# The first two matrices of a batched matmul loaded as one DMA of 4 KB runs each, instead of two DMAs of 2 KB and 6 KB runs

## Chip, cores, metric

One core of a Trainium2 chip. The metric is the device time of one execution in microseconds; lower is better. "Faster" and "slower" mean over 2%.

## The reference

```python
batch, m, k, n = 16, 512, 512, 512
a: [batch, k, m] float32      b: [batch, k, n] float32
np.matmul(a.transpose(0, 2, 1), b).astype(np.float32)
```

## The kernel before

Each matrix is 1 MB. The sync engine (SP) issues all transfers into one queue that is served by 16 DMA engines. The first batch element is loaded alone so that compute can start early, and each of its two matrices comes in two DMAs: the top 128 rows, one 2 KB row for a partition, then the other 384 rows, three rows (6 KB) for a partition. The second element follows in 8 KB runs, the rest in pairs of elements, 2 MB a DMA, 16 KB runs. VectorE casts to bf16, TensorE multiplies, ScalarE evicts, and SP issues the stores after the loads. Cut to the parts that matter:

```python
in0_v = [x.rearrange("batch (p r) m -> batch p r m", r=RV) for x in (a, b)]          # RV = 4
top_v = [x[0][0:P].rearrange("p m -> p () m") for x in (a, b)]                        # P = 128
low_v = [x[0][P:K].rearrange("(p r) m -> p r m", r=RV - 1) for x in (a, b)]
# ... (cut: tiles and semaphores)
for j in range(2):
    nc.sync.dma_start(x_ts[j][:, 0:1, :], top_v[j]).then_inc(s_f[j], 16)
    nc.sync.dma_start(x_ts[j][:, 1:RV, :], low_v[j]).then_inc(s_f[j], 16)
for j in range(2):
    nc.sync.dma_start(x_ts[j][:, RV:R, :], in0_v[j][1]).then_inc(s_x[j], 16)
for n in range(2, 2 * pairs):
    if n >= NX:                                     # NX = 4 input buffers
        nc.sync.wait_ge(s_in, n - NX + 1)           # wait until the buffer has been cast
    # ... (cut: the load of matrix pair n; the last one in two halves, s_h and s_x)
nc.sync.wait_ge(s_h, 16)
for i in range(pairs - 1):
    nc.sync.wait_ge(s_out, i + 1)
    nc.sync.dma_start(out_v[i], o_ts[i % NO][:]).then_inc(s_o if i else s_o0, 16)

for u in range(G):                                  # the first two batch elements
    if u:
        nc.vector.wait_ge(s_mm, H)
    for j, bf_ts in enumerate((abf_ts, bbf_ts)):
        nc.vector.wait_ge(s_x[j] if u else s_f[j], 16 if u else 32)
        nc.vector.tensor_copy(
            out=bf_ts[0][:], in_=x_ts[j][:, u * RV:(u + 1) * RV, :]
        ).then_inc(s_cast, 1)
        # ... (cut)
# ... (cut: later casts, matmuls, evictions, last store)
```

Any order of the 512 rows over partitions and slots is right, as long as a and b use the same one, because the rows are summed over.

## Time and profile before

| | kernel before |
|---|---|
| time, median of 3 runs | 123.50 us (123.36 to 123.52) |
| span of the profiled execution | 122.1 us (its time 123.84) |
| share of DMA engines' time taken | 97.3% |
| cast of the first a / first b starts | 5.82 / 8.95 us |
| first matmul | 10.47 us |
| last landing of the first b | 8.93 us |

The lines of the profile are shown in the prediction. Some words: a run of memory is a contiguous piece that is moved in one go, and a packet is the record of one such move on one DMA engine. A stall is the time by which a packet lasts longer than is usual for its size. A DMA is issued when SP starts it, and lands when its last share has been counted; the line is what has been issued and not yet moved. A reload is a load into an input buffer that is used a second time. In tables of windows the two last columns are the busy share of the DMA engines and the GB/s that they moved; GB/s times a window of 1 us gives kB.

### The profile page before, as it was taken

How to read it: one execution, taken by the hardware profiler on the slowest of the kernel's cores; microseconds unless marked ns; L12 is line 12 of the kernel's file. 1: busy time of each engine (PE TensorE's matmuls, PEld its weight loads, DVE VectorE, ACT ScalarE, POOL GpSimd, SP SyncE). 2: the span in 40 equal slices, each digit the busy share in tenths (PEclk: the TensorE clock that was granted, in tenths of full speed). 3: DMA queues.
4: the chain of work that ended last, by engine and by line, in shares of the span. 5: the costliest groups of instructions: out<-in, count | busy, mean ns of one | idle time of the engine just before them, and what ended most of it. 6: DMA issues, size and time to landing. Idle time of an engine off the chain costs nothing.

```text
span 122.1 us, 1209 instructions
## 1 busy us (share of the span) xinstructions
PE 62.1 (51%) x480; PEld 35.0 (29%) x480; DVE 38.1 (31%) x48; ACT 32.2 (26%) x41; POOL 0.2 (0%) x4
## 2 busy tenths in 40 slices
PE   0005928379969749979919928989900000000000
PEld 0002304035546325636606605646500000000000
DVE  0033070680494092474356437492000000000000
ACT  4000332400570840091470290091570000000000
POOL 0000000000000000000000000000000000000000
PEclk9999999959999985999999999999997555555555
DMA  2999999999999999999999999999999999999993
GB/s 86 375 411 429 454 429 435 435 440 435 429 429 429 429 429 429 429 429 435 429 429 435 429 429 416 421 429 427 427 421 429 427 429 427 429 429 424 427 429 145
DMA packets 5200, 50.33 MB, mean 412 GB/s; under 512 B 464, under 2 KB 464, under 8 KB 976
## 3 DMA queue, kind: packets, MB, share of 16 engines
q1 hardware_dynamic: 5200, 50.33, 97.3%
HBM read 33.55 MB, written 16.78 MB: 412 GB/s over the span
## 4 chain that ended last, share of the span: by engine, by line
DMA 43%; DVE 7%; ACT 3%; PE 3%; issue 3%; ACTq 0%
DMA x<-in_b_dram 37%; DMA out_dram<-o 6%; DVE abf L117 4%; ACT o L180 3%; DVE bbf L117 3%; PE ps L135 3%; DVE done L123 0%; ACTq L72 0%
## 5 line engine op out<-in xcount | busy, mean ns | idle before, releaser
L155 PE MATMUL ps<-bbf,abf 64*128 64x512 bf16 x448 | 52.9, 393 | 13.1 <-PEq L150 13.1
L155 PEld LDWEIGHTS ps<-bbf,abf 64*128 64x128 bf16 x448 | 31.2, 113 | 34.8 <-issue 20.0
L180 ACT COPY o<-ps 128x1024 f32<-128x1024 f32 x28 | 26.3, 1026 | 40.5 <-PE ps L155 36.5
L117 DVE CAST abf<-x 128x2048 bf16<-128x2048 f32 x14 | 17.1, 1224 | 17.4 <-PE ps L155 13.3
L117 DVE CAST bbf<-x 128x2048 bf16<-128x2048 f32 x14 | 17.1, 1225 | 14.2 <-DMA x<-in_b_dram 14.2
L135 PE MATMUL ps<-bbf,abf 128*128 128x512 bf16 x32 | 9.2, 451 | 13.2 <-PEq L133 13.2
L135 PEld LDWEIGHTS ps<-bbf,abf 128*128 128x128 bf16 x32 | 3.8, 123 | 18.1 <-issue 16.1
L174 ACT COPY o<-ps 128x1024 f32<-128x1024 f32 x4 | 4.1, 1014 | 17.2 <-PE ps L135 17.2
L98 DVE CAST abf<-x 128x2048 bf16<-128x2048 f32 x2 | 2.5, 1227 | 11.7 <-PE ps L135 5.9
L98 DVE CAST bbf<-x 128x2048 bf16<-128x2048 f32 x2 | 2.5, 1225 | 1.9 <-DMA x<-in_b_dram 1.9
L185 ACT ACTIVATE done<-done 1x1 uint32<-1x1 uint32 x8 | 1.6, 196 | 0.0
L174 ACT ACT_TABLE_LOAD x1 | 1.3, 1283 | 0.9 <-SPq L72 0.9
L123 DVE MEMSET done<- 1x1 f32 x14 | 0.8, 59 | 0.0
L102 DVE MEMSET done<- 1x1 f32 x2 | 0.1, 59 | 0.0
L207 POOL MEMSET const-bfloat16-1.0<- 128x1 bf16 x1 | 0.1, 102 | 0.0
L207 POOL MEMSET const-uint8-127<- 128x1 uint8 x1 | 0.1, 102 | 0.0
L207 POOL MEMSET const-float32-0.0<- 128x1 f32 x1 | 0.1, 99 | 0.2 <-issue 0.2
L207 POOL MEMSET const-float32-1.0<- 128x1 f32 x1 | 0.1, 99 | 0.0
## 6 DMA issues: line engine op xcount, KB each, us to landing
out_dram<-o SPq DMA_DIRECT2D x8, 2048.0 KB, 21.8
x<-in_a_dram SPq DMA_DIRECT2D x7, 2048.0 KB, 12.1
x<-in_b_dram SPq DMA_DIRECT2D x6, 2048.0 KB, 15.9
x<-in_b_dram SPq DMA_DIRECT2D x3, 1024.0 KB, 13.4
x<-in_a_dram SPq DMA_DIRECT2D x1, 1024.0 KB, 8.6
x<-in_a_dram SPq DMA_DIRECT2D x1, 768.0 KB, 4.4
x<-in_b_dram SPq DMA_DIRECT2D x1, 768.0 KB, 6.6
x<-in_a_dram SPq DMA_DIRECT2D x1, 256.0 KB, 2.8
```

Source lines behind the costliest of these rows:

```text
L98: nc.vector.tensor_copy(out=bf_ts[0][:], in_=x_ts[j][:, u * RV:(u + 1) * RV, :]).then_inc(s_cast, 1)
L102: nc.vector.memset(dve_done[:, j:j + 1], 0.0).then_inc(s_in, 1)
L117: nc.vector.tensor_copy(out=(bbf_ts if n % 2 else abf_ts)[v][:], in_=x_ts[n % NX][:, v * RV:(v + 1) * RV, :],).then_inc(s_cast, 1)
L123: nc.vector.memset(dve_done[:, n:n + 1], 0.0).then_inc(s_in, 1)
L135: mm = nc.tensor.matmul(ps_ts[0][h][:, t % 2, :], a_m[:, r, t], bbf_ts[0][:, r, :], start=(r == 0), stop=(r == RV - 1),)
L155: mm = nc.tensor.matmul(ps_ts[g][h][:, t % 2, :], a_m[:, t], bbf_ts[v][rows, r, :], start=(v == 0 and r == 0), stop=(v == V - 1 and r == R ...
L174: nc.scalar.copy(out=o_ts[0][:, g, 2 * h:2 * h + 2, :], in_=ps_ts[0][h][:]).then_inc(s_ev[h], 1)
L180: ev = nc.scalar.copy(out=o_ts[i % NO][:, g, 2 * h:2 * h + 2, :], in_=ps_ts[g][h][:])
L185: nc.scalar.memzero(act_done[:, i:i + 1]).then_inc(s_out, 1)
L207: nc = _bacc.Bacc("TRN2", target_bir_lowering=False, num_devices=1)
```

## The change

The intent: no 2 KB packets at the start, two issues and two completions less, and the shorter of the first runs twice as long (2 to 4 KB; the longer ones shrink from 6 to 4 KB). Each matrix is split into an upper and a lower half of 256 rows; a partition takes two rows (4 KB) of each.

```diff
-    top_v = [x[0][0:P].rearrange("p m -> p () m") for x in (a, b)]
-    low_v = [x[0][P:K].rearrange("(p r) m -> p r m", r=RV - 1) for x in (a, b)]
+    first_v = [x[0].rearrange("(h p r) m -> p h r m", h=2, p=P) for x in (a, b)]
...
-            nc.sync.dma_start(x_ts[j][:, 0:1, :], top_v[j]).then_inc(s_f[j], 16)
-            nc.sync.dma_start(x_ts[j][:, 1:RV, :], low_v[j]).then_inc(s_f[j], 16)
+            nc.sync.dma_start(
+                x_ts[j][:, 0:RV, :].rearrange("p (h r) m -> p h r m", h=2), first_v[j]
+            ).then_inc(s_f[j], 16)
...
-                nc.vector.wait_ge(s_x[j] if u else s_f[j], 16 if u else 32)
+                nc.vector.wait_ge(s_x[j] if u else s_f[j], 16)
```

## The prediction

> **What bounds the kernel now.** I read the views in this order: the busy shares and the DMA queue line, the chain of waits, the waits of the queue that issues the transfers, then a table of windows over the first microseconds and the rest. The page says first:
>
> ```profile
> span 122.1 us, 1209 instructions
> PE 62.1 (51%) x480; PEld 35.0 (29%) x480; DVE 38.1 (31%) x48; ACT 32.2 (26%) x41; POOL 0.2 (0%) x4
> DMA  2999999999999999999999999999999999999993
> DMA packets 5200, 50.33 MB, mean 412 GB/s; under 512 B 464, under 2 KB 464, under 8 KB 976
> q1 hardware_dynamic: 5200, 50.33, 97.3%
> ```
>
> No compute engine is busy for much over half the span; the 16 DMA engines are busy for 97.3% of it, and 38 of the 40 slices are full. The traffic is 50.33 MB and cannot shrink. The chain ends like this:
>
> ```profile
> 66.05 13.45 DMA x<-in_b_dram
> 79.50 0.02 issue
> 79.51 7.35 DMA out_dram<-o
> 86.86 0.02 issue
> 86.88 3.76 ACT o L180 x4
> 90.64 0.06 ACTq L72
> ```
>
> The chain stops at 90.64 us, where the last store is issued, but the span ends at 122.1. The landing view gives 30.3 us from issue to landing for that last 2 MB store, which at 429 GB/s needs 4.9 us by itself: the other 25 us it stands in line behind earlier stores. So the chain's casts, matmuls and evictions do not set the end; the amount of work in the DMA line does. Nor does the line run dry earlier: the first reload (issued 17.34 us, landed near 28.4) takes 11 us from issue to landing, of which 4.9 is its own transfer and 1.2 the start-up (first issue 0.94 us, first packet 2.18), so some 5 us of other work still lay ahead of it, and the later ones (up to 19.3 us) have more. A load that is issued a microsecond earlier or later changes nothing at the end. Only these terms count: when the first packet starts, how long each DMA engine then needs for its fixed list of packets, and the last landing.
>
> The change touches the first 2 MB only. The windows there, and after:
>
> ```profile
> 2.00:3.00 1.00, 0.00 (x0) 0.00 (x0) 0.00 (x0) 0.18 (x1) 0.00 (x0) 1.00 0.71 231
> 3.00:4.00 1.00, 0.00 (x0) 0.00 (x0) 0.00 (x0) 0.00 (x0) 0.00 (x0) 1.00 0.99 363
> 4.00:5.00 1.00, 0.00 (x0) 0.00 (x0) 0.00 (x0) 0.00 (x0) 0.00 (x0) 1.00 1.02 422
> 5.00:6.00 1.00, 0.00 (x0) 0.00 (x0) 0.18 (x1) 0.00 (x0) 0.00 (x0) 1.00 1.09 356
> 6.00:7.00 1.00, 0.00 (x0) 0.00 (x0) 1.00 (x1) 0.00 (x0) 0.00 (x0) 1.00 0.89 369
> 7.00:8.00 1.00, 0.00 (x0) 0.00 (x0) 0.04 (x1) 0.00 (x0) 0.00 (x0) 1.00 1.04 430
> 8.00:9.00 1.00, 0.00 (x0) 0.00 (x0) 0.05 (x1) 0.00 (x0) 0.00 (x0) 1.00 1.06 442
> ...
> 24.00:79.00 55.00, 43.93 (x370) 26.06 (x372) 28.00 (x36) 19.10 (x25) 0.00 (x0) 0.94 1.00 430
> 79.00:119.00 40.00, 8.99 (x82) 5.14 (x77) 3.61 (x5) 7.64 (x10) 0.00 (x0) 0.67 1.01 428
> ```
>
> The last column is GB/s, the one before it the busy share. The first packet starts at 2.18, so up to 9.00 the queue has 6.82 us and moves 231+363+422+356+369+430+442 = 2613 kB. At 429 that would take 6.09 us. **0.73 us is all that the beginning loses** against the steady rate, busy share near 1 all the while: packets take longer there, they are not missing. This is the prize, and it is 0.6% of the time.
>
> The trace records each packet too (no view lists them; I counted the records). Undisturbed, one engine starts its next packet 80 ns after a 2 KB packet began, 231 after 6 KB, 306 after 8 KB, and 6 ns after a semaphore packet. The cost fits 4.7 ns + 75.3 ns for each 2 KB. Over that, some packets stall: the second packets of eight engines at the start (208 to 325 ns instead of 84), the first 6 KB packets of a on five engines near 3.0 us (546 to 613 instead of 234), and those of b on seven engines from 5.65 us (416 to 1013). Summed over the medians and divided by 16 engines: 0.12 us in the 2 KB packets, 0.31 us in the 6 KB packets. Most of the rest is that eight of the engines get their first packet 0.26 us after the other eight. Two engines come out late: for b's 6 KB transfer 14 of the 16 landings are in by 8.49 us, the last at 8.93, and on the very last store it is 120.72 against 121.16. Those 0.44 us are carried to the end of the kernel by engines that each have an equal list.
>
> **The Trainium skill.** "DMA: Bandwidth & Descriptors", section "Why small descriptors are slow (HBM only)": a fixed cost of about 3 cycles for each packet. The trace agrees in kind: 4.7 ns a packet here, 6% of a 2 KB one, 2% of a 6 KB one. "Perfetto Trace Analysis", section "DMA Optimizations": merging transfers of small runs, such as 2 KB into 4 or 8 KB, can raise throughput dramatically. This is the intent of the change, but in this trace a 2 KB packet moves 2048 B in 80 ns, so 16 engines 410 GB/s, and only 256 of 5200 packets are of that kind. The first page's section "Latency and other measured facts" has about 600 ns to the first byte of a hardware-issued DMA; here it is 1.24 us from the start of the issue, 0.85 from its end. Its section "Specifications" has 435 GB/s for the fabric and about 358 for a core's share of HBM; the trace holds 428 to 430, so the first is the ceiling here.
>
> **The change part by part.** Two issues go: four of 128 runs become two of 256 runs. An issue costs 0.39 to 0.43 us, and a store with 256 runs (two of 8 KB a partition) shows 0.40 at its cheapest, so the count of runs hardly matters; the later loads are issued about 2 x 0.47 = 0.94 us earlier. They join a full line, so this is worth 0 at the end. Two completion counts go: 2 x 16 semaphore packets, on each engine 2 x 6 = 12 ns, on the path. The packets: each engine carries 8 partitions; before, a partition of one matrix costs 80 + 231 = 311 ns, after it 2 x (4.7 + 150.6) = 311 ns. **The number of runs stays at two in a partition and so does the number of bytes; the longer short run is paid by the shorter long run.** 16 x 0 = 0. Sum of what is certain: -0.01 us.
>
> What is not certain is the stalls. Three of the five starts of a new region (a's lower rows, b's upper and lower) are merged into starts of whole matrices, so the 0.31 us mean of the 6 KB packets, and the 0.44 us of the two late engines, may go in part. Afterwards each matrix still has a first touch of both halves, and the next loads (8 KB) show 0.03 us mean excess, so first touches need not be dear. I choose half: -0.2 us. Against it, if runs are handed out at a fixed pace, the second eight engines get their first packet 0.5 instead of 0.26 us late: +0.1 us for an even chance. Together some -0.15 to -0.2 us.
>
> The first casts should start earlier (a 5.82 to about 5.5 us, b 8.95 to about 8.5), and the first matmul at about 10.0 instead of 10.47. All of this is beside the full DMA line.
>
> **Rivals.** (1) All stalls go with the small and the second transfers: the beginning reaches the steady rate, -0.6 us, 122.9. For it: the stalls sit exactly on the transfers that are merged. Against it: the very first packets stall too, and a start remains. (2) Stalls are as large with two regions half a matrix apart, visited in turn, and the 256 runs start slower: +0.2 to +0.5 us, 123.7 to 124. For it: every engine touches both regions at once; against it: the stores too have two runs a partition, 1 MB apart, and run at 428 GB/s. (3) The earlier first matmul carries through to the end: -0.5 us and more. Against it: the line never runs dry after 2.18 us, and the last store waits 25 us in it. (4) The skill's sentence on small runs taken at face value, a gain in per cent: even free 2 KB packets would give 256 x 80 ns / 16 = 1.3 us, 1%.
>
> **Range and chances.** Before, three runs lie within 0.16 us, so the stalls repeat rather than being chance. 123.5 - 0.2 gives 123.3. No rival that I can size goes past 2.47 us (2%) to either side: the whole startup loss is 0.73 us. Range 122.7 (all stalls gone, and a little) to 123.7 (rival 2, small). Faster by over 2%: 0.01; slower: 0.01; within: 0.98.
>
> **What would show it right or wrong.** Right: 5168 packets, of them 432 under 512 B and 944 under 8 KB; the queue's share still 97%; windows after 9 us at 428 to 430 GB/s; casts of a and b up to half a microsecond earlier without the end following by more than the gain in bytes moved by 9 us. Wrong: a window below 420 GB/s after 10 us, or a first packet later than 2.5 us, or 4 KB packets that take other than some 159 ns, or reloads that now land in under 7 us from their issue, so that the line ran short.

## The result, and the profile after

The changed kernel took 123.48 us (median of 4 runs, 123.31 to 123.61), the kernel before in the same rounds 123.51 (123.36 to 123.54). The ratio is 0.9999, 95% interval 0.9982 to 1.0016: the same. A ratio here is the mean time of one kernel's fast runs over the mean of the other's fast runs of the same rounds, so it is not quite the ratio of the two medians. Executions over 1.5% slower than the fastest of the same kernel are left out of the means.

The profile page of the changed kernel, its span, DMA row, packets and queue share:

```profile
span 121.5 us, 1207 instructions
DMA  2999999999999999999999999999999999999994
DMA packets 5168, 50.33 MB, mean 414 GB/s; under 512 B 432, under 2 KB 432, under 8 KB 944
q1 hardware_dynamic: 5168, 50.33, 97.7%
```

The packet counts are the expected ones: 32 semaphore packets less, and the same number of data packets. The windows of the changed kernel, columns as before:

```profile
2.00:3.00 1.00, 0.00 (x0) 0.00 (x0) 0.00 (x0) 0.18 (x1) 0.00 (x0) 1.00 0.79 152
3.00:4.00 1.00, 0.00 (x0) 0.00 (x0) 0.00 (x0) 0.00 (x0) 0.00 (x0) 1.00 0.93 381
4.00:5.00 1.00, 0.00 (x0) 0.00 (x0) 0.00 (x0) 0.00 (x0) 0.00 (x0) 1.00 1.01 418
5.00:6.00 1.00, 0.00 (x0) 0.00 (x0) 0.13 (x1) 0.00 (x0) 0.00 (x0) 1.00 1.03 422
6.00:7.00 1.00, 0.00 (x0) 0.00 (x0) 1.00 (x1) 0.00 (x0) 0.00 (x0) 1.00 1.02 422
7.00:8.00 1.00, 0.00 (x0) 0.00 (x0) 0.10 (x1) 0.00 (x0) 0.00 (x0) 1.00 1.13 467
8.00:9.00 1.00, 0.00 (x0) 0.00 (x0) 0.64 (x1) 0.00 (x0) 0.00 (x0) 1.00 1.02 434
...
24.00:79.00 55.00, 44.61 (x375) 26.56 (x377) 27.47 (x37) 19.56 (x26) 0.00 (x0) 0.94 1.01 430
```

From 9 us on little differs (435 and 432 GB/s up to 24 us, 430 in both up to 79). Before that, two things moved in opposite directions:

- **The start is slower.** By 3.0 us the change has moved 152 kB, the kernel before 231. The packet records show why: sixteen 4 KB packets start by 2.24 us, eight of them last 661 to 858 ns instead of 159, and the next packet starts at 2.73. Before, packets flow from 2.44 us on; 58 had started by 2.7 us. The 79 kB are 0.18 us at 429 GB/s.
- **The middle is faster.** From 3 to 9 us the change moves 2544 kB, the kernel before 2382 in its first profile. The stalls of the first 6 KB packets are gone: between 3.5 and 9 us no packet lasts over its usual time. The 162 kB are 0.38 us.

So in this pair of profiles the change is ahead by 0.19 us at 9 us. The first a, which takes the slow start in full, is cast at 5.87 us instead of 5.82; b at 8.36 instead of 8.95; the first matmul comes at 9.88 instead of 10.47. The two late engines are gone as well: on the last store all 16 landings lie between 120.17 and 120.59. The other 0.4 us of the span difference (122.1 against 121.5) are about what these late engines were late by (0.44). But the times do not show 0.57 us, so the two profiles had to be doubted first.

### The profile page after: what moved, and what is told of

Read it like the earlier page. It is cut to its first block, busy times and chain, and to the rows that moved or that the text cites. A ratio compares the mean times of both kernels' runs of the same rounds, so it can differ in the third digit from the quotient of the medians.

```text
span 121.5 us, 1207 instructions
## 1 busy us (share of the span) xinstructions
PE 61.9 (51%) x480; PEld 35.1 (29%) x480; DVE 38.1 (31%) x48; ACT 32.2 (26%) x41; POOL 0.2 (0%) x4
## 2 busy tenths in 40 slices
DMA packets 5168, 50.33 MB, mean 414 GB/s; under 512 B 432, under 2 KB 432, under 8 KB 944
## 3 DMA queue, kind: packets, MB, share of 16 engines
q1 hardware_dynamic: 5168, 50.33, 97.7%
## 4 chain that ended last, share of the span: by engine, by line
DMA 59%; DVE 6%; issue 3%; ACT 3%; SPq 2%; ACTq 0%
DMA x<-in_b_dram 53%; DMA out_dram<-o 6%; ACT o L180 3%; DVE bbf L117 3%; DVE abf L117 3%; SPq L77 1%; SPq L73 1%; SPq L83 1%; DVE done L123 0%; ACTq L71 0%; SPq L218 0%; SPq L71 0%
```

## The experiments

Twelve runs follow, of eight further kernels and of the two of the change; each was correct. The main theory, S: the change trades stalls in the middle for a pause at the start, and the pause comes from the 256 runs of the first DMA. One number recurs, the kB moved in windows: "start" is from 2 to 3 us, "by 9" from 2 to 9 us. In some expectations I spoke of "the second eight engines" starting late; the records do not name the engine of a packet, and kB at the start is the sounder measure.

### Again: the changed kernel and the kernel before, unaltered

> The changed kernel once more, for a second profile and more timed rounds. Theory S (the start eats the gain): the change trades the stalls in the middle of the first 2 MB for a dearer start, because 256 runs are handed out more slowly than 128. It expects the second eight engines to get their first packet again about 0.70 us after the first eight (0.26 in the kernel before), the 4 KB packets to stall only in the first microsecond, and the ratio to the kernel before within 0.998 to 1.002. Theory C (chance): the stalls of both kernels are chance and say nothing of the change; it expects them in other places or of other sizes than in the first profile.

Measured: 123.29 us against 123.53; ratio 0.998 (0.9953 to 1.0008). All first sixteen packets last 671 to 922 ns, the seventeenth starts at 2.85 us; start 131 kB, by 9: 2704; no stall over 0.1 us from 3.5 to 9 us. The pause and the calm afterwards repeat; the prediction's even-chance term of 0.1 us was a term that is always there.

> The kernel before, one more look. If the stalls in the middle of its first 2 MB come from its four DMAs for the first matrices, packets stall again at the first 6 KB packets near 3.0 and 5.7 us, by some 0.2 to 0.8 us each, on several engines. If they were chance, they are gone or stand elsewhere. Profiled span 121.5 to 122.4.

Measured: one execution of 123.39 us, span 121.6. Its windows:

```profile
2.00:3.00 1.00, 0.00 (x0) 0.00 (x0) 0.00 (x0) 0.18 (x1) 0.00 (x0) 1.00 0.72 223
3.00:9.00 6.00, 0.00 (x0) 0.00 (x0) 1.98 (x2) 0.00 (x0) 0.00 (x0) 1.00 1.03 412
```

That is 2695 kB by 9 us. Stalls stand at the same places again (3.0 to 3.2, 5.65 to 6.1 us), but smaller: at most 0.26 us there, against 0.78 in the first profile; one of 0.30 us stands elsewhere, at 4.50. No engine left the first loads late: b's last landing came at 8.22 us, and b was cast at 8.24. **So these places belong to the kernel, and the size of the stalls differs from one execution to the next**; the first profile of the kernel before was an unlucky one. By 9 us this execution had moved as much as the changed kernel. Most of the 0.57 us between the first two profiles was not the change.

The very start differs too, and this limits theory S: the first eight packets of the kernel before took 0.63 to 0.64 us here (0.61 with the hold below), where the first profile has 0.08 to 0.10. Long first packets are thus not peculiar to the change. What is peculiar to it is that the other packets wait as well; here they go on from 2.43 us.

> The changed kernel once more, for its ratio on the same chip as the other runs of this call. Pause at the start to 2.7 to 2.9 us, no stalls of over 0.1 us from 3.5 to 9 us, b cast at 8.2 to 8.4 us, ratio to the kernel before 0.997 to 1.000.

Measured: 123.33 us against 123.52; ratio 0.9988 (0.9974 to 1.0003); start 98 kB, by 9: 2671, one stall of 0.20 us where I had expected none over 0.1, b cast at 8.44. The three ratios of the changed kernel, 0.9999, 0.998 and 0.9988, all have intervals that hold 1.

### The size of the runs and their number, apart

> 4 KB runs as in the change, but each matrix in two DMAs of 128 runs (upper and lower half): the run size of the change without its merging. Theory S: the start is as in the kernel before (second eight 0.26 us late), since the first DMA has 128 runs; if the stalls in the middle come from the start of a further DMA, 4 KB packets stall again near 3 and 5.5 us by 0.2 to 0.7 us each, and the ratio is 0.998 to 1.002. Rival: the stalls in the middle came from the mix of 2 KB and 6 KB runs; then none is seen there, and the ratio is 0.995 to 0.998.

```diff
+            for h in range(2):
+                nc.sync.dma_start(
+                    x_ts[j][:, 2 * h:2 * h + 2, :], first_v[j][h]
+                ).then_inc(s_f[j], 16)
```

(in place of the one DMA, with first_v indexed by half, and the wait for 32). The windows of this kernel:

```profile
2.00:3.00 1.00, 0.00 (x0) 0.00 (x0) 0.00 (x0) 0.18 (x1) 0.00 (x0) 1.00 0.97 299
...
5.00:6.00 1.00, 0.00 (x0) 0.00 (x0) 0.54 (x1) 0.00 (x0) 0.00 (x0) 1.00 0.97 291
6.00:7.00 1.00, 0.00 (x0) 0.00 (x0) 0.69 (x1) 0.00 (x0) 0.00 (x0) 1.00 0.99 360
```

Measured: 124.06 us (123.39 to 124.38), ratio 1.0021 (0.9988 to 1.0055). The data packets are those of the change, the same bytes in the same 4 KB runs; a DMA has 128 of them instead of 256, one in a partition instead of two, so their order differs too. The start has 299 kB: **the pause is gone**, 50 packets started by 2.7 us where the change has 16. In its place four packets near 5.0 us stall by 0.96 to 1.5 us, larger than I had expected (0.2 to 0.7), and the window from 5 to 6 us drops to 291 GB/s with the busy share still at 0.97. The mix of 2 KB and 6 KB runs is therefore not what makes packets stall. Nor do longer runs help: this is 4 KB throughout, and it is no faster than 2 KB plus 6 KB.

> First a and b in one DMA each, 512 runs of 2 KB. Theory S paced by the number of runs: the second eight engines start about 1.4 us after the first eight; the packets cost 8 x 4 x 80 = 2.56 us a matrix on an engine instead of 2.49; b is cast at about 9.0 us; ratio 1.002 to 1.008. Rival B, paced by bytes: the second eight start about as late as with 4 KB runs or earlier (0.3 to 0.7 us), ratio 1.000 to 1.003.

```diff
+    first_v = [x[0].rearrange("(r p) m -> p r m", p=P) for x in (a, b)]
...
+            nc.sync.dma_start(x_ts[j][:, 0:RV, :], first_v[j]).then_inc(s_f[j], 16)
```

Measured: 123.94 us (123.86 to 123.95), ratio 1.0027 (1.0 to 1.0054); start 125 kB, by 9: 2590; b cast at 8.95. 31 packets start by 2.48 us, all have ended by 2.56, and the next starts at 2.73. The pause is there with 512 runs, as engines that have nothing to do (busy share 0.37 in this window), and ends at the same time as with 256. So it is not proportional to the count: my 1.4 us failed. It is there with 256 and 512 runs, and not with 128; but those are also the kernels with two and four runs in a partition instead of one, so the count of runs and the form of the DMA are not told apart. The ratio and b's time came as expected.

> First a and b in one DMA each, 128 runs of 8 KB. Theory S with a hand-out paced by the number of runs: the second eight engines start about 0.26 us after the first as in the kernel before, b is cast at about 8.0 us (8.36 after, 8.95 before), the profiled span some 0.3 us under that of the changed kernel, the ratio to the kernel before 0.995 to 0.999. Rival B, paced by bytes or by the first touch of the memory: the second eight start 0.7 to 1.3 us late, nothing is won, ratio 0.999 to 1.004.

```diff
-    first_v = [x[0].rearrange("(h p r) m -> p h r m", h=2, p=P) for x in (a, b)]
...
+            nc.sync.dma_start(x_ts[j][:, 0:RV, :], in0_v[j][0]).then_inc(s_f[j], 16)
```

Measured: 123.26 us, ratio 0.9971 (0.9944 to 0.9998). By 3.0 us 254 kB against the change's 152, so no pause:

```profile
2.00:3.00 1.00, 0.00 (x0) 0.00 (x0) 0.00 (x0) 0.18 (x1) 0.00 (x0) 1.00 0.71 254
3.00:4.00 1.00, 0.00 (x0) 0.00 (x0) 0.00 (x0) 0.00 (x0) 0.00 (x0) 1.00 0.89 352
```

The second line shows what it pays: some forty small stalls of 0.04 to 0.3 us up to 5.7 us. By 9: 2711. b was cast at 8.34 us, where I had expected 8.0. The ratio came as expected, the 0.3 us off the profiled span did not (121.9, in an execution that took 123.62, the slowest of its six).

> One DMA of 128 runs of 8 KB for each first matrix again, beside the changed kernel. If it is better than the change by the pause at the start alone (0.5 us on every engine), its times lie 0.2 to 0.4 us under after_third. If, as in its first run, many small stalls up to 6 us take the place of the pause, both are equal within 0.15 us.

Measured on one chip with the third run of the change: 123.22 us against its 123.33; ratio to the kernel before 0.9976 (0.9961 to 0.9990). The second branch of the expectation holds: the two differ by 0.11 us. It is the best version that I found, 0.3 us under the kernel before in both runs, and by the measure of 2% still the same. Both intervals lie below 1, as the one of the 2 KB runs lies above or at it: from 1024 runs of 2 KB to 256 of 8 KB the time falls by 0.68 us (123.94 to 123.26). By the packet times of the prediction, 64 x 80 against 16 x 306 ns on an engine, an estimated 0.22 us of this is the packets' own cost.

### One part alone

> One part of the change alone: b in one DMA of two 4 KB runs a partition, a in two DMAs of 128 runs of 4 KB (the same order of rows). Theory: no pause at the start, since the first DMA has 128 runs (about 50 packets started by 2.7 us, 16 in the changed kernel), and no stalls of over 0.4 us near 5 us, since b's second DMA is gone; a is cast at about 5.4 us, b at about 8.1, ratio to the kernel before 0.994 to 0.998. Rival: the first packets of b stall whether b comes in one DMA or two, as b's first half did in the kernel with two DMAs each (1.0 to 1.5 us near 5 us); then b is cast at 8.6 us or later and nothing is won over the change.

```diff
+            if j:
+                nc.sync.dma_start(
+                    x_ts[j][:, 0:RV, :].rearrange("p (h r) m -> p h r m", h=2), first_v[j]
+                ).then_inc(s_f[j], 16)
+            else:
+                nc.sync.dma_start(x_ts[j][:, 0:2, :], up_v).then_inc(s_f[j], 16)
+                nc.sync.dma_start(x_ts[j][:, 2:RV, :], dn_v).then_inc(s_f[j], 16)
```

(and the cast of a waits for 32). Measured: 124.36 us (123.28 to 124.98), ratio 1.0069 (1.0031 to 1.0107). The start is the best of all, 377 kB, and a is cast at 5.39 us. But the first packets of b stall near 5.0 us by 0.55 to 0.65 us, four of them, although b comes in one DMA, and b is cast at 8.60. The theory falls: b's second DMA is not what stalls; the rival holds. The profiled execution took 123.51 us; no profile was taken of one near 125, so that these longer ones had larger stalls is likely from the kernel with two DMAs each, but not shown.

### Are later issues to blame?

> The kernel before, with the issue of the two 2 MB loads that follow held until the first b has landed (8.9 us; 2 MB are then still in line, so the line does not run dry). Theory D (a further DMA's start stalls, whatever else is issued): the stalls near 3.0 and 5.7 us stay as they are. Rival I (the stalls come from descriptors of later DMAs being written while the engines work): those near 5.7 us go, the profiled span falls by 0.2 to 0.4 us, ratio 0.997 to 0.999. A ratio above 1.004 would mean that the line ran short.

```diff
+        nc.sync.wait_ge(s_f[1], 32)
         for n in range(2, 2 * pairs):
```

Measured: 123.53 us, ratio 1.0007 (0.9984 to 1.0030). Five packets near 5.65 us stall by 0.28 to 0.86 us although nothing was issued between 3.8 and 8.8 us. Rival I falls for the stalls near 5.65 us; those near 3.0 come while the second element's loads are issued (2.80 to 3.78 us) in this kernel too, and are not tested.

> The changed kernel with everything behind the first a and b held until the first a has landed (5.9 us; b is then still in line). Theory S, in which the 256 runs of the first DMA themselves make the pause at the start: the gap between the first sixteen packets and the next, to about 2.75 to 2.85 us, stays, ratio to before 0.997 to 1.001. Rival I: the pause comes from the issues that follow at 1.9 to 4.1 us, and goes; then a is cast at about 5.3 instead of 5.8 us and the ratio is 0.993 to 0.997.

```diff
+        nc.sync.wait_ge(s_f[0], 16)
         for j in range(2):
             nc.sync.dma_start(x_ts[j][:, RV:R, :], in0_v[j][1]).then_inc(s_x[j], 16)
```

Measured: 123.99 us, ratio 1.0042 (1.0019 to 1.0066). The start has 127 kB and a is cast at 5.92 us: the pause stays, with only a's and b's own DMAs issued. Rival I falls there too. The ratio missed, and usefully: the loads of the second element are issued at 5.9 us, 1.9 us before their turn, and nine of their first packets stall at 7.8 to 8.1 us by 0.13 to 0.46 us; their last landing moves from 13.26 to 13.71 us. With these issues held back the kernel takes 0.4% longer than the kernel before. That the short notice makes the stalls is not shown: in the kernel with two DMAs each, where these loads were issued at 2.80 us, seven of their first packets stall too, by 0.16 to 0.21 us.

### Does the line of transfers alone set the end?

> The changed kernel with the first cast held until the second b has landed (13.3 us instead of 5.9): the first matmul comes some 4.5 us later, at about 14.5. If the line of transfers alone sets the end and has some 5 us of other work ahead of the first reload, as predicted, the time changes by less than 0.3%; the first reload is then issued near 21 us and lands at about the same time as before (27.8 us). If the first casts mattered for the end, the ratio to the kernel before would be up to 1.036.

```diff
+        nc.vector.wait_ge(s_x[1], 16)      # s_x[0] in the other of the two
         for u in range(G):
```

Measured: 126.15 to 130.19 us in four executions, of which two, the profiled one among them, count as slow for their times (the clock is the same, 0.85); the ratio of the two others is 1.0282 (1.0221 to 1.0343), slower. The first reload was issued at 23.65 us, 7.3 us later than in the changed kernel, not the 4.6 I had reckoned, because the stages behind the first matmul moved too. The line had run out at 22.6 us. The experiment overshot; it says only that a reload issued after the line has run dry costs.

> The changed kernel with the first cast held until the second a has landed (10.8 us instead of 5.9). The hold to 13.3 us put the first reload's issue at 23.7, past the end of the line's work (22.6 us), so my 5 us of spare were overdrawn by the 7.3 us that the reload moved. Held to 10.8, the reload should be issued near 20 us, some 3.5 us later than without the hold, its first packets some 1.2 us after that, 1.4 us before the line runs out. If the line alone sets the end, the ratio to the kernel before is 0.997 to 1.002 although the first matmul comes 3.5 us later; if early compute matters, 1.02 or more.

The line and the windows of this kernel:

```profile
20.16 0.33 SPq L83 DMA_DIRECT2D x<-in_a_dram  x1
```

```profile
22.50:23.50 1.00, 1.00 (x7) 0.49 (x6) 0.00 (x0) 0.03 (x1) 0.00 (x0) 1.00 0.77 295
...
80.00:90.00 10.00, 9.34 (x84) 5.49 (x80) 3.60 (x5) 5.62 (x7) 0.00 (x0) 1.00 0.93 385
```

The same windows of the changed kernel:

```profile
22.50:23.50 1.00, 0.00 (x0) 0.00 (x0) 0.68 (x2) 0.03 (x1) 0.00 (x0) 1.00 0.96 410
...
80.00:90.00 10.00, 7.47 (x68) 4.33 (x64) 2.52 (x5) 6.03 (x9) 0.00 (x0) 1.00 1.02 430
```

Measured: 125.68 us (124.85 to 126.38), ratio 1.0180 (1.0136 to 1.0223): by the measure of 2% unclear, and between the two branches of the expectation. The reload was issued at 20.16 us, near what I expected, 2.6 us before the landing of what stood ahead of it. And 14 of its 16 landings came by 27.71 us, no later than in the changed kernel (27.79). But its first packets stalled, by up to 1.3 us, and one engine's share landed at 29.73. That engine stayed 1.9 us late until the last load. The stores wait for loads to land, so SP issued them at 80.82 instead of 78.91 us, the other engines ran out of work, and the second pair of windows shows the 10% missing there. The expectation failed: this reload, issued 2.6 us before its turn, was not free. In the trace the loss goes through the one late engine: 14 landings of the last load were in by 78.89 us, the last at 80.81, and the stores were issued right after it. But this is one profile, and the time alone does not exclude that early compute matters.

## Why the prediction was right, and where its steps were not

**The time.** 123.3 predicted, 123.48 measured, range 122.7 to 123.7. The three ratios, 0.9999, 0.998 and 0.9988, put it 0.0 to 0.25 us below the kernel before, where the prediction had it 0.2; weighted by their intervals they give an estimated 0.9991, 0.1 us, and the interval (0.9981 to 1.0001) still holds 1. So a gain of 0.2 us is neither shown nor excluded. The chances were right for the reason given: no bytes and no runs are saved, and the whole start had only 0.73 us to give.

**The packets.** 5168, 432 and 944 are as predicted, and a 4 KB packet takes 159 ns. "16 x 0 = 0" holds. The kernel of 4 KB runs in two DMAs agrees: longer first runs, no gain. The later loads were issued 0.86 us earlier, the last of them 0.56, not 0.94, because issues took up to 0.61 us; as predicted, nothing followed from it at the end.

**The start.** This is the mis-sized term. The prediction gave the slower start 0.1 us, at an even chance. It is there in every profile of the change: 98, 131, 152, and 127 kB with the hold, against 223 to 231 kB before, 0.17 to 0.31 us at 429 GB/s. The first cast of a came at 5.87 us (5.71 and 5.94 in the repeats), not at the predicted 5.5; where the start had no pause and a came in 4 KB runs, it came at 5.39 and 5.46. Rival 2 was right in kind, but the change got back in the middle what it lost here.

**The middle.** The prediction took half of the stalls away. In the changed kernel nearly all went (at most one of 0.2 us between 3.5 and 9 us), so this term was too small, by about as much as the other. The means of the profiles (three of the change, two of the kernel before) are 127 against 227 kB at the start, a loss of 0.23 us at 429 GB/s, and 2563 against 2427 kB from 3 to 9 us, a gain of 0.32: 0.08 us ahead at 9 us. That two wrong sizes nearly cancelled, so that the sum came out close, was luck. The prediction's statement that the stalls repeat rather than being chance, read from three times within 0.16 us, holds for their places but not for their sizes: over its later rounds the kernel before spread from 123.17 to 124.21, and two profiles of it had 0.78 and 0.30 us as the largest stall after 3 us. The engines that were late all through the first profile go with the large stalls: in the second profile none was late at 9 us, with the hold three were, by 0.3 to 0.4 us.

**The spare time.** The step "a load that is issued a microsecond earlier or later changes nothing" stands for this change, whose reload came 1.0 us earlier (16.38 instead of 17.34), but "some 5 us" of spare was too generous: 3.8 us later the time was already 1.8% longer. Where between the two the cost begins was not tried.

**What stays open.** What makes the first packets stall in the middle. It is not the mix of run sizes and not a second DMA for b, and near 5.65 us not issues that come later. Large stalls appear, in some executions, in the kernels whose first DMA starts without a pause and is followed by a second for a; they are small with one DMA of 128 runs and nearly absent behind a pause. That is a pattern of these runs, not a cause. Nor do they say why a first DMA of 256 or 512 runs pauses until about 2.7 to 2.9 us. That the count of runs makes the pause, as theory S has it, is argued: in every kernel here a higher count went with more than one run in a partition, and no run parted the two.

## What to carry to other kernels

When a queue is full from the first microsecond to the last, a change of run lengths is worth what the packet costs add up to: here a 4 KB pair costs just what 2 KB plus 6 KB cost, because the count is the same. For the first transfer of this kernel, one run for each partition started without a pause of all engines, and two or four did not. Before explaining half a microsecond between two profiles, take each a second time: one kernel differed from itself by as much.

## What the Trainium skill lacked or had wrong

- "DMA: Bandwidth & Descriptors": it has a first-byte latency of about 600 ns for hardware-issued DMAs, which fits the 0.63 to 0.85 us from the end of the first issue to the first packet here (1.0 to 1.2 us from its start), but no figure for what follows the first packets. Here a first DMA of 256 or 512 runs moved 98 to 156 kB from 2 to 3 us, one of 128 runs 223 to 377 kB.
- "Perfetto Trace Analysis", section "DMA Optimizations": "(e.g., 2KB → 4KB or 8KB) can dramatically improve throughput". One engine starts a packet every 80 ns for 2 KB, 155 for 4 KB and 306 for 8 KB, so 16 engines reach 410, 423 and 428 GB/s: under 5% from end to end. For the first two matrices, the step from 2 KB to 8 KB runs took 0.68 us off the whole kernel, 0.5%; the start, 125 against 254 kB from 2 to 3 us, is in this figure.
- No page has a figure for how long one engine's stall is carried on. Here a late engine stayed late, which fits 16 engines that each have an equal list: 0.44 us were carried from 9 us to the end in the first profile, and 1.9 us from 29.7 to 80 us when the casts were held.
- No page says how many microseconds ahead of its turn a transfer should be issued to a busy queue: with 1.9 us nine first packets stalled by up to 0.46 us, and with about 2.6 us one engine lost nearly 2 us. One profile each, so this is a lead and not a rule.
